# One two-layer mixer and expert kernel, its engines' work ordered by the list scheduler's timeline model instead of its coarse one

## The chip, the cores and the metric

The kernel runs on one core of a Trainium2 chip. The time is device microseconds of one execution; a smaller number is better. The core has a matmul engine (TensorE, in the rows PE, with PEld for its weight loads), VectorE (DVE), ScalarE (ACT), GpSimd (POOL) and SyncE (SP), which here only issues the DMA transfers. Each engine works through its own list of instructions in the order in which the built program holds them, and waits on semaphores where it needs another engine's result or a buffer.

## The reference

256 tokens `x` and 256 context tokens `ctx` of width 1024 run through two layers. Everything is float32.

```
for l in range(DEPTH):                      # 2 layers
    hl = _modulate(xl, norm1_g[l], shift, scale)     # the same for ctx
    pl = _split((hl @ w_in).astype(jnp.float32), IN_SIZES)
    a_l, a_c = _deltanet_branch(...)        # A: 4 heads, chunks of 64, triangular solve, scan both ways
    b_l, b_c = _gla_branch(...)             # B: 4 heads, chunks of 16, decays, scan both ways
    d_l, d_c = _diff_branch(...)            # C: softmax attention, p[0] - lam * p[1]
    y = (ga * (ya @ w_o_a) + gb * (yb @ w_o_b) + gd * (yd @ w_o_c)) @ w_out
    xl = xl + mod * y
    # layer 0: swiglu(h, w1, w3, w2), width 2816
    # layer 1: 8 experts of width 2816, the best 2 of each token
return _rmsnorm(xl, final_g)
```

## The kernel before

Activations lie with the model's width on the partitions, 512 tokens (context and `x`) beside each other. Weights come from HBM in pieces of 0.5 to 1 MB (`load`, L241 to L249) and are split for float32 accuracy: ScalarE copies the high part (L267), VectorE subtracts it to get the low part (L268), and a product is three matmuls (`mm3`, L272 to L274): high by high, high by low, low by high. In the first layers the two parts live in a tile `whl`, of which there are six; in the expert stage they are called `whi`, `wlo` and `wp`.

The function `mixer` writes the branches in the order of a plan, one string for each layer, for instance for layer 0:

```
"sm ap su pr iv ga4 m4 za sc m16 dec qkB gb1 ha ma vB gla qC kC m4 gc1 vC hb dif mb hc mc"
```

Here `ap`, `pr`, `iv` and `sc` are branch A: projections, preparation (`E` at L618, `U` at L622), the inverse of the triangular 32x32 blocks, and the scan over chunks. `iv` holds a chain of 31 steps on VectorE alone:

```
for c in range(31):
    a, b = 31 - c, c + 1
    nc.vector.tensor_mul(tv, N[:, c + 1:, c:c + 1]..., Y[:, c:c + 1, :b]...)   # L653
    nc.vector.tensor_sub(Y[:, c + 1:, :b], Y[:, c + 1:, :b], tv)               # L655
```

`gla` is branch B: eight iterations (four chunks of 128 tokens, two directions). Each builds decay factors (`F` on TensorE at L947 and L948, exponentials `Fe` on ScalarE at L950, products `zq` at L973 and `Fe` at L976 on VectorE), small matmuls `la` (L985), masked copies `ATb` from PSUM on VectorE (L987), and the outputs `ob` (L996, L998). `dif` is branch C, 16 heads of attention in layer 0 (scores at L1052, maxima at L1053, exponentials at L1056). The letters `g`, `z`, `h`, `m` and `m4` stand for gates, output gates, the output norm of a branch, its merge, and units of the modulation vectors (L348, L366): work of large projections that the branches don't wait for. In the text it is called filler, and so are the projections of the next branch (`qkB`, `vB`, `qC`, `kC`, `vC`).

The program order is only a priority. [...] After the mixer follow the dense layer (`ffn`) or, in layer 1, the experts (`turn` L1349 to L1356): 8 experts of 11 steps, each of which fetches 3 MB, casts it in six pieces on ScalarE and VectorE, and multiplies.

## Time and profile before

| what | value |
|---|---|
| median of 3 runs | 2604.94 us (2601.87 to 2605.57) |
| the profiled execution | 2607.5 us, its span 2605.7 us |
| busy share of the span | PE 94%, DVE 66%, ACT 54%, POOL 3% |
| mean granted TensorE clock | 0.962 of full |

The page lists for each engine its busy time, a picture of the span in 40 slices, and the chain of work that ended last. [...] A filler group of 24 matmuls of 512 columns needs two pairs of casts; TensorE works through it in about 5.4 us (24 by 227 ns) while the casts go on for the next.

### The profile page before, as it was taken

What the parts mean: (1) busy time and instruction counts of PE and PEld (TensorE: products, weight loads), DVE (VectorE), ACT (ScalarE), POOL (GpSimd) and SP (SyncE); (2) the same over time, 40 slices, a digit from 0 to 9 for tenths busy, and PEclk for the clock granted to TensorE, in tenths of its full rate; (3) what the DMA queues carried; (4) which work ended last, traced back from release to release, by engine and by line L of the source; (5) the groups of instructions that cost most, each with busy time, mean ns of one, the idle gap of its engine ahead of it and who ended that gap; (6) DMA issues with size and microseconds to landing.
All of it is one profiled execution on the core that took longest, in us unless ns stands there. A gap on an engine that the chain in (4) does not pass through costs nothing.

```text
span 2605.7 us, 35872 instructions
## 1 busy us (share of the span) xinstructions
PE 2455.8 (94%) x13712; PEld 1979.8 (76%) x13712; DVE 1718.3 (66%) x3130; ACT 1417.3 (54%) x2352; POOL 87.6 (3%) x216
## 2 busy tenths in 40 slices
PE   5998999999998999998979999998999999999997
PEld 3786777677677788886859878787878888878876
DVE  4675446655644533335686475767988888988987
ACT  3764343225553432334845432666878777777775
POOL 0000001110010000000000010010000000000000
PEclk8998999989999999998978999998999999999998
DMA  6323632022132223222273130246979899999994
GB/s 248 110 93 149 246 132 71 17 106 81 49 128 83 81 77 121 96 74 89 97 271 115 46 141 33 89 169 261 386 270 365 332 350 351 346 347 353 342 366 181
DMA packets 72707, 473.13 MB, mean 182 GB/s; under 512 B 8208, under 2 KB 10384, under 8 KB 19664
## 3 DMA queue, kind: packets, MB, share of 16 engines
q1 hardware_dynamic: 68208, 464.73, 48.1%
q10 hardware_dynamic: 4320, 6.03, 0.6%
q8 instruction: 110, 1.80, 0.3%
q14 instruction: 69, 0.57, 0.1%
HBM read 463.65 MB, written 7.08 MB: 181 GB/s over the span
## 4 chain that ended last, share of the span: by engine, by line
PE 85%; DVE 8%; ACT 4%; issue 2%; DMA 1%; SPq 0%; POOL 0%; ACTq 0%; DVEq 0%; POOLq 0%
PE pm L273 19%; PE pm L272 19%; PE pm L274 19%; PE y L274 3%; PE y L273 3%; PE y L272 3%; PE la L985 2%; PE pm L348 2%; PE pq L1052 1%; DVE ATb L987 1%; PE pm L844 1%; PE ob L996 1%; PE tp L1352 1%; DMA raw<-in_wmod_dram 1%; DVE zq L973 1%
## 5 line engine op out<-in xcount | busy, mean ns | idle before, releaser
L268 DVE TENSOR_TENSOR whl<-raw,whl 128x512 fp32r<-128x512 f32 (+2 forms) x490 | 331.2, 682 | 341.0 <-ACT whl L267 338.0
L272 PE MATMUL pm<-hh,whl 128*128 128x512 f32 (+2 forms) x1264 | 477.7, 380 | 13.0 <-ACT whl L267 6.6
L274 PE MATMUL pm<-hh,whl 128*128 128x512 f32 (+2 forms) x1264 | 467.7, 371 | 12.3 <-DVE whl L268 12.3
L267 ACT CAST whl<-raw 128x512 fp32r<-128x512 f32 (+2 forms) x490 | 289.8, 600 | 339.9 <-PE pm L274 268.7
L273 PE MATMUL pm<-hl,whl 128*128 128x512 f32 (+2 forms) x1264 | 470.9, 373 | 0.0
L268 DVE TENSOR_TENSOR wp<-rawc,wp 128x1024 fp32r<-128x1024 f32 x261 | 313.6, 1222 | 36.7 <-ACT wp L267 30.6
L272 PEld LDWEIGHTS pm<-hh,whl 128*128 128x128 f32 (+1 forms) x1264 | 244.8, 194 | 60.6 <-ACT whl L267 8.6
L274 PEld LDWEIGHTS pm<-hh,whl 128*128 128x128 f32 (+1 forms) x1264 | 243.5, 193 | 54.8 <-DVE whl L268 14.3
L267 ACT CAST wp<-rawc 128x1024 fp32r<-128x1024 f32 x261 | 268.1, 1051 | 21.1 <-PE y L274 11.5
L273 PEld LDWEIGHTS pm<-hl,whl 128*128 128x128 f32 (+1 forms) x1264 | 244.7, 194 | 42.6 <-issue 6.3
L268 DVE TENSOR_TENSOR wlo<-raw,whi 128x1024 fp32r<-128x1024 f32 x176 | 210.0, 1222 | 34.1 <-ACT whi L267 31.6
L273 PE MATMUL pm<-wlo,hg 128*128 128x512 f32 x530 | 211.8, 400 | 1.6 <-DVE wlo L268 1.4
L272 PE MATMUL pm<-whi,hg 128*128 128x512 f32 x530 | 211.2, 398 | 0.0
L274 PE MATMUL pm<-whi,hg 128*128 128x512 f32 x530 | 207.7, 392 | 0.0
L267 ACT CAST whi<-raw 128x1024 fp32r<-128x1024 f32 x176 | 179.0, 1052 | 13.2 <-PE pm L273 11.9
L273 PE MATMUL y<-wp,mt 128*128 128x512 f32 x348 | 135.4, 389 | 0.0
L274 PE MATMUL y<-wp,mt 128*128 128x512 f32 x348 | 135.3, 389 | 0.0
L273 PEld LDWEIGHTS pm<-wlo,hg 128*128 128x128 f32 x530 | 99.7, 188 | 34.6 <-DVE wlo L268 15.8
L272 PE MATMUL y<-wp,mt 128*128 128x512 f32 x348 | 120.1, 389 | 0.2 <-ACT mt L1354 0.2
L272 PEld LDWEIGHTS pm<-whi,hg 128*128 128x128 f32 x530 | 99.7, 188 | 20.9 <-ACT hg L1328 0.2
L274 PEld LDWEIGHTS pm<-whi,hg 128*128 128x128 f32 x530 | 99.7, 188 | 20.2
L268 DVE TENSOR_TENSOR wlo<-rawc,whi 128x1024 fp32r<-128x1024 f32 x91 | 110.9, 1219 | 1.9 <-ACT whi L267 1.3
(394 smaller groups left out, 4542.8 us busy)
## 6 DMA issues: line engine op xcount, KB each, us to landing
rawc<-in_m_dram SPq DMA_DIRECT2D x176, 1024.0 KB, 6.0
raw<-in_m_dram SPq DMA_DIRECT2D x88, 1024.0 KB, 7.4
raw<-in_win_dram SPq DMA_DIRECT2D x64, 1024.0 KB, 4.9
raw<-in_wmod_dram SPq DMA_DIRECT2D x40, 1024.0 KB, 5.0
raw<-in_f_dram SPq DMA_DIRECT2D x22, 1024.0 KB, 4.8
raw<-in_wo_dram SPq DMA_DIRECT2D x24, 512.0 KB, 3.7
raw<-in_f_dram SPq DMA_DIRECT2D x16, 704.0 KB, 4.0
rawc<-in_wmod_dram SPq DMA_DIRECT2D x8, 1024.0 KB, 16.9
```

Source lines behind the costliest of these rows:

```text
L267: self.nc.scalar.copy(hi, src)
L268: self.nc.vector.tensor_sub(lo, src, hi.bitcast(F32))
L272: mm(p, wh, ah, start=first, stop=False)
L273: mm(p, wh, al, start=False, stop=False)
L274: mm(p, wl, ah, start=False, stop=last)
L348: nc.tensor.matmul(p[j:j + 32, :256], self.cs[:, k, o:o + 32], w[:, k], start=i == 0 and k < 4, stop=i == n - 1 and k >= 4)
L844: nc.tensor.matmul(ps[:, :n], self.ones, sq[:, :n], start=True, stop=True)
L973: nc.vector.tensor_mul(FQ[hp][r, x, a].rearrange("p (n s) -> p n s", s=LEVELS[li]), side(Fj[:, x]), side(q[hp]))
L985: mm(p[:, x % 2, hp], FK[hp][:, x], FQ[hp][:, x], start=True, stop=True)
L987: nc.vector.copy_predicated(AT.rearrange("p h a (n t s) -> p (h a) n t s", t=2, s=s)[:, :, :, 1 - d], mk[:, None].to_broadcast([128, 4, 64 ...
L996: mm(o[:, hp], vB[:, tt, h * 128:(h + 1) * 128], AT[:, hp, a], start=True, stop=first)
L1052: mm(p[:, :nk], q[ms, h, cs], k[ms, h, :nk], start=True, stop=True)
```

## The change

One argument of the scheduler's context is set. The list scheduler then orders all engines' work with its timeline model (a time for every instruction, engine by engine) in place of its coarse one. The program handed to it, its priorities, buffers and instructions are the same; TensorE, VectorE, ScalarE and GpSimd have the same instructions before and after, in another order, and only the waits between engines are placed anew.

```
@@ -1565,7 +1565,7 @@
     out = nc.dram_tensor("out_0_dram", (128, 8, 256), F32, kind="ExternalOutput").ap()
-    with tile.TileContext(nc) as tc:
+    with tile.TileContext(nc, schedule_with_timeline_sim=True) as tc:
         program(tc, args, out)
```

Three places of the new order follow. The first is VectorE in `iv` of layer 0, the chain of L653 and L655. Before, its last steps and what stands behind it:

```order
L653 TENSOR_TENSOR fs<-W_1173 128x60
L655 TENSOR_TENSOR W_1173<-W_1173,fs 128x2x30
L653 TENSOR_TENSOR fs<-W_1173 128x31
L268 TENSOR_TENSOR whl<-raw,whl 128x512
L655 TENSOR_TENSOR W_1173<-W_1173,fs 128x31
L268 TENSOR_TENSOR whl<-raw,whl 128x512 x2
L658 COPY_PREDICATED W_1172<-mk,W_1173 128x1024
```

With the change the middle of the same chain reads so:

```order
L655 TENSOR_TENSOR W_1173<-W_1173,fs 128x22x10
L268 TENSOR_TENSOR whl<-raw,whl 128x512
L653 TENSOR_TENSOR fs<-W_1173 128x231
L268 TENSOR_TENSOR whl<-raw,whl 128x512 x2
L655 TENSOR_TENSOR W_1173<-W_1173,fs 128x21x11
L268 TENSOR_TENSOR whl<-raw,whl 128x512
L653 TENSOR_TENSOR fs<-W_1173 128x240
```

Before, one filler cast stands inside the 31 steps, just ahead of the last; with the change eight stand inside them, and three results of the gate `zs` (L807) too.

The second place is VectorE in an iteration of `gla` in layer 0, the seventh of eight. Before:

```order
L268 TENSOR_TENSOR whl<-raw,whl 128x512
L987 COPY_PREDICATED ATb<-mk,la 128x4x64
L268 TENSOR_TENSOR whl<-raw,whl 128x512
L973 TENSOR_TENSOR zq<-Fe,qkB 64x64 x7
L976 TENSOR_TENSOR Fe<-Fe,qkB 128x384
L973 TENSOR_TENSOR zq<-Fe,qkB 64x64 x5
L268 TENSOR_TENSOR whl<-raw,whl 128x512
L976 TENSOR_TENSOR Fe<-Fe,qkB 128x384
```

With the change:

```order
L973 TENSOR_TENSOR zq<-Fe,qkB 64x64 x6
L987 COPY_PREDICATED ATb<-mk,la 128x4x64
L976 TENSOR_TENSOR Fe<-Fe,qkB 128x384
L973 TENSOR_TENSOR zq<-Fe,qkB 64x64 x6
L976 TENSOR_TENSOR Fe<-Fe,qkB 128x384
L987 COPY_PREDICATED ATb<-mk,la 128x8x32
L987 COPY_PREDICATED ATb<-mk,la 128x16x16
```

The casts are gone from the last four iterations: the filler they belong to has been placed in the first four, and none is left. TensorE's list says the same: at the outputs of the fourth iteration it has 46 us more filler behind it than before (matmuls counted in both lists, at the start-to-start times of the trace, 227 ns for 512 columns and 120 ns for 256), and then no group until `gla` has ended.

The third place is ScalarE in the experts, one step of the sixth. `mt` (L1354) and `ms` (L1344) are the activations of the step, `whi` and `wp` weight casts. Before:

```order
L1354 CAST mt<-tp 128x256
L267 CAST wp<-rawc 128x1024 x2
L1344 ACTIVATE ms<-pm 128x256
L267 CAST wp<-rawc 128x1024
L267 CAST whi<-rawc 128x1024
L1328 CAST hg<-pm 128x512 x2
L267 CAST whi<-raw 128x1024 x2
```

With the change:

```order
L1354 CAST mt<-tp 128x256
L267 CAST whi<-raw 128x1024 x2
L1344 ACTIVATE ms<-pm 128x256
L1328 CAST hg<-pm 128x512 x2
L267 CAST wp<-rawc 128x1024 x3
L267 CAST whi<-rawc 128x1024
```

The pair of casts from `raw` moves from the end of the step to its start.

## Rows read from the trace of the kernel before

**Rows 1.** The page: busy time by engine, the chain that ended last.

```profile
PE 2455.8 (94%) x13712; PEld 1979.8 (76%) x13712; DVE 1718.3 (66%) x3130; ACT 1417.3 (54%) x2352; POOL 87.6 (3%) x216
...
PE 85%; DVE 8%; ACT 4%; issue 2%; DMA 1%; SPq 0%; POOL 0%; ACTq 0%; DVEq 0%; POOLq 0%
```

**Rows 2.** Windows of the span, from:to, length, busy by engine, PEclk, DMA share, GB/s.

```profile
150.00:200.00 50.00, 46.26 (x282) 37.19 (x281) 44.39 (x117) 27.12 (x42) 0.00 (x0) 0.99 0.33 114
200.00:250.00 50.00, 40.74 (x585) 32.90 (x582) 30.76 (x61) 27.55 (x44) 1.81 (x1) 0.84 0.29 108
...
900.00:1000.00 100.00, 100.00 (x443) 82.81 (x442) 36.74 (x61) 30.55 (x55) 0.00 (x0) 1.00 0.24 83
...
1350.00:1400.00 50.00, 38.04 (x635) 31.87 (x628) 38.96 (x82) 27.37 (x49) 1.81 (x1) 0.69 0.55 201
...
2400.00:2500.00 100.00, 99.33 (x456) 80.28 (x455) 90.60 (x102) 73.97 (x94) 0.00 (x0) 1.00 0.94 353
```

**Rows 3.** Timeline around the end of the inverse, layer 0 (start, us, what).

```profile
206.58 0.69 DVE L268 TENSOR_TENSOR whl<-raw,whl 128x512 fp32r<-128x512 f32 x1
...
207.32 0.80 PE L274 MATMUL pm<-hh,whl 128*128 128x512 f32 x1 [3.50 <-DVE whl L268]
```

**Rows 4.** Timeline of TensorE in the inverse of layer 1.

```profile
1367.80 0.58 PE L274 MATMUL pm<-hh,whl 128*128 128x256 f32 x1 [3.95 <-DVE whl L268]
```

**Rows 5.** Windows of `gla`, layer 0: four iterations, then single ones.

```profile
345.00:488.50 143.50, 133.69 (x722) 104.76 (x722) 85.78 (x251) 51.46 (x110) 13.41 (x58) 0.96 0.25 85
488.50:508.90 20.40, 19.42 (x104) 14.27 (x104) 15.47 (x56) 4.58 (x12) 3.68 (x15) 1.00 0.00 0
508.90:530.90 22.00, 19.51 (x141) 13.20 (x140) 13.49 (x50) 4.77 (x12) 3.02 (x14) 1.00 0.26 99
530.90:564.50 33.60, 32.55 (x147) 24.71 (x148) 19.16 (x62) 12.90 (x25) 3.42 (x15) 0.80 0.36 132
564.50:582.40 17.90, 16.59 (x117) 14.85 (x117) 11.57 (x44) 3.61 (x8) 2.31 (x10) 1.00 0.04 16
```

**Rows 6.** Groups of VectorE instructions, 345 to 584 us (busy, mean ns).

```profile
L973 DVE TENSOR_TENSOR zq<-Fe,qkB 64x64 f32<-64x64 f32 x224 | 40.8, 217 | 6.9 <-ACT Fe L950 2.6 <-PE tp L956 1.7 <-PE la L985 1.4
L987 DVE COPY_PREDICATED ATb<-mk,la 128x256 f32<-128x256 uint8 x56 | 29.1, 519 | 15.8 <-PE la L985 15.4
L268 DVE TENSOR_TENSOR whl<-raw,whl 128x512 fp32r<-128x512 f32 x40 | 27.1, 689 | 24.8 <-ACT whl L267 24.3
L976 DVE TENSOR_TENSOR Fe<-Fe,qkB 128x384 f32<-128x384 f32 (+1 forms) x48 | 22.2, 463 | 0.8
```

**Rows 7.** Chain of work at the end of the iteration 508.9 to 530.9.

```profile
525.59 0.47 DVE Fe L976
526.05 0.27 DVE zq L973 x2
...
527.58 0.47 PE la L985 x2
...
528.07 0.44 DVE ATb L987
...
530.07 0.73 DVE ATb L987
```

**Rows 8.** Groups of instructions in `dif`, layer 0, 600 to 725 us.

```profile
L1053 DVE TENSOR_REDUCE r<-pq 128x1 f32<-128x256 f32 (+1 forms) x32 | 17.2, 554 | 17.9 <-PE pq L1052 17.9
L1062 DVE SCALAR_TENSOR_TENSOR e<-e,r 128x256 f32<-128x256 f32 (+1 forms) x16 | 9.9, 616 | 0.4
...
L1056 ACT ACTIVATE e<-pq,r 128x256 f32<-128x256 f32 (+1 forms) x32 | 18.4, 579 | 17.1 <-DVE r L1054 17.1
```

**Rows 9.** Expert steps: the transposes L1352 of two stretches, first and last start.

```profile
L1352 PE MATMUL tp<-cstt,ms x19: 270/271/272, 1849.8 to 1925.6; 128*128 128x128 f32 x19
...
L1352 PE MATMUL tp<-cstt,ms x18: 270/271/272, 2512.9 to 2582.2; 128*128 128x128 f32 x18
```

**Rows 10.** Waits in the experts, 1850 to 2590 us (us, times, longest).

```profile
ACT ms L1344 <- PE pm L274: 76.9, 66, 2.4
...
PEld pm L273 <- DVE wlo L268: 15.8, 41, 0.9
```

**Rows 11.** VectorE's largest group in the experts (busy, mean ns).

```profile
L268 DVE TENSOR_TENSOR wp<-rawc,wp 128x1024 fp32r<-128x1024 f32 x244 | 292.9, 1222 | 31.5 <-ACT wp L267 26.4
```

More of the change, by code (lines that the diff above doesn't have):

```diff
@@ L1567 @@
     out = nc.dram_tensor("out_0_dram", (128, 8, 256), F32, kind="ExternalOutput").ap()
-    with tile.TileContext(nc) as tc:
+    with tile.TileContext(nc, schedule_with_timeline_sim=True) as tc:
         program(tc, args, out)
```

## The prediction

> **What bounds the kernel now.** I read the page first. TensorE is busy for 2455.8 of 2605.7 us and holds 85% of the chain that ended last, VectorE 8%, ScalarE 4% [rows 1]. An order can't take matmuls away, so all that it can win is the 150 us in which TensorE is idle, and what the lower clock costs. Next I read the windows, which say where these lie. The dense layer has no gap at all (100.00 of 100, clock 1.00), and the experts have next to none (99.33 of 100) [rows 2]. The losses sit in the mixers: around the inverse of branch A (40.74 of 50 us at clock 0.84 in layer 0, 38.04 at 0.69 in layer 1) [rows 2] and in `gla` [rows 5], where long chains on VectorE leave TensorE only filler. So the question is where the new order puts the filler, and I compared, at each milestone on TensorE, the filler that stands ahead of it in the two lists.
>
> **The inverse, layer 0.** Before, TensorE waits 3.50 us for a cast that VectorE does only at the end of its 31-step chain [rows 3], and then works on at the lower clock. With the change eight casts stand inside the chain, so this wait should go. The price: the chain becomes longer by 8 casts of 0.69 us [rows 6], and by three gates of about the same, some 7.5 us, and the join and the scan behind it come later by as much. Moreover TensorE's list has 12 to 19 us more filler ahead of the preparation, so that the chain also starts later. That is no loss by itself, since the filler has to be done at some time; but it is then missing behind the chain, in the first half of the scan. The window of the inverse loses 50 - 40.74 = 9.3 us of idle time and up to 0.16 x 50 = 8 us by the clock [rows 2], so at best 8 to 10 us come back of these 17; at worst the scan gets the same gaps (10 us more). I take **+2** (-8 to +10), nearer to the balance, since the gaps are moved rather than filled. In layer 1 the same wait (3.95 us) stands in the same place [rows 4], and the same move is made, with less filler left for the scan: **0** (-10 to +8).
>
> [...]
>
> **`gla`, layer 0.** This is the largest term. Eight iterations take 345 to 582 us. Before, each has 4 to 11 us of filler between its own steps, and some 15 us are left behind them. With the change the first four have all of it (46 us more than before, counted in the two lists), the last four have none. The last four took 20.4 + 22.0 + 33.6 + 17.9 = 93.9 us [rows 5]. What would they take bare? VectorE's own work is, for one iteration, 28 `zq` of 0.217, 7 `ATb` of 0.519 and 6 `Fe` of 0.463 us, 6.1 + 3.6 + 2.8 = 12.5 us [rows 6], and 1 us of small pieces, so 13.5; four are 54 us, the lower bound. The nearest measured iteration with little filler is the one of 508.9 to 530.9: about 4 us of filler and 22.0 us [rows 5]; the chain at its end goes from VectorE to TensorE and back, neither of them full [rows 7]. Four such are 88 us, the upper bound. The last iteration took 17.9 us with 8 us of filler, with TensorE busy for 16.59 of them [rows 5]; bare it can't be slower than that unless the clock falls, which makes 72. I take 76, a little above, because TensorE's own share (16.59 - 8 = 9 us of an iteration) leaves it idle for half of the time, and the clock fell right after the gaps of the iteration at 508.9: 0.80 in the next [rows 5].
>
> Against that stand the 46 us of filler and 4 us of modulation units that the last four no longer hold or that no longer follow them, and the stalls which the first four lose: 143.5 - 133.69 = 9.8 us idle and 0.04 x 143.5 = 5.7 us of clock [rows 5], of which I count 8. The old stretch with its filler behind it is 93.9 + 15 = 109 us, of which 50 move forward; so the bare four replace 59 us, and the term is 76 - 59 - 8 = **+9** (54 gives -13, 88 gives +21).
>
> [...]
>
> **`dif`, layer 0.** The filler there is also pulled forward, by up to 28 us: the last 7 of the 16 heads have no cast between them. A head needs on VectorE 2 x 0.554 + 0.616 + some 1.0 for its small pieces, 2.7 us, on ScalarE 2 x 0.579 and copies, 2.1 us [rows 8], and on TensorE about 3.4 us (its matmuls in the list at the trace's durations). TensorE would stay the bound of a bare head, if the heads overlap; the 17.9 us that `L1053` waits for scores and the 17.1 that the exponentials wait for maxima [rows 8] say that they overlap only in part. Seven heads at 0 to 1.2 us of gap: **+4** (0 to +8). For `gla` and `dif` in layer 1 the shift is smaller (only the last iteration of `gla` is bare): **+1** (-5 to +7).
>
> **The dense layer** keeps TensorE's order, row for row: 0. The first 60 us change a little, with loads in the same order: 0 (2 to either side).
>
> **The experts.** In the first experts a step takes (1925.6 - 1849.8) / 9 = 8.42 us, in the last one (2582.2 - 2512.9 - 0.3) / 8 = 8.63 [rows 9]. TensorE works all the time in the former; the latter carry a wait of `wlo`, 41 times and 15.8 us in all [rows 10], while VectorE is busy for 90.60 of 100 us [rows 2] with casts of 1222 ns [rows 11]. With the change the casts from `raw` come directly behind `mt`. Counted over the stage in the two lists, between the matmul that frees a cast's buffer and the one that first reads the new cast stand 6 to 7 us of matmuls in the median, where 4.1 to 4.5 stood. So most of the wait should go: 41 waits at 8.63 - 8.42 = 0.21 us of step each make 8.6. The new order is less regular, and `ms` on ScalarE, which already waits 76.9 us for its matmuls [rows 10], now has other casts queued behind it, which can cost a new wait. I take **-8** (-12 to +6).
>
> **The sum.** +2 + 0 + 9 + 4 + 1 - 8 = +8 us on the profiled 2607.5, 2615.5. The median of the runs shown is 2.6 us below that execution, so I forecast 2613.
>
> **The rivals.** *The bare tails run at VectorE's bound, and the covered chains pay* (the other side). The place is the last four iterations of `gla`: if the decay products, which don't depend on the scan's state, are ordered ahead well enough to keep VectorE full, they take 54 to 56 us instead of 76; the sum becomes 8 - 21 = -13 and the time 2592. It decides from about 67 us for the four downwards, where the sum is -1. For it: VectorE's order in these iterations has the `zq` of two groups in one run (x12). Against it: the 15.8 us in which `ATb` waits for `la` [rows 6]. *The bare tails lose the clock*: the four take 88 us (+21), `dif` +8, one inverse +6, experts -6: 2605 + 30 = 2635. For it: 0.80 and 0.69 after such gaps [rows 5, 2]; against it: the iteration at 508.9, which had the gaps, still ran at 1.00 itself [rows 5]. *No measurable change*: the gains of the experts and of the inverse equal the tails, or the chip's queues even it out, 2600 to 2610. For it: the dense layer and the experts, two fifths of the span, run at TensorE's own pace in either order.
>
> **How the numbers follow.** I give the forecast's case 0.36, the fast tails 0.28, the slow clock 0.19 and no change 0.17. About 0.2% (5 us) is what a measurement of this kernel can tell from no change. Of the forecast's case, whose own range is 2603 to 2625, about four fifths are slower by more than that and the rest is no change; so slower is 0.29 + 0.19 = 0.48, no change 0.07 + 0.12 = 0.19, faster 0.28 and 0.05 of the last case that falls below, 0.33. The range takes in most of both outer cases: 2584 to 2638.
>
> **What would show it.** Right: the wait of 3.5 us in the inverse is gone; the last four iterations of `gla` have no `whl` cast and TensorE busy for about half; `dif` ends with seven bare heads; the expert steps are 8.42 us to the end. Wrong: if the four bare iterations take under 65 us, or if the filler put ahead leaves new gaps in the scan or at the ends of branches, which I priced at little, or if the new order of the experts brings waits in place of the old ones; a step at 8.8 us there would alone cost 15 us.

## The result: 4.6% slower, and the profile after

With the change the kernel takes 2723.46 us (median of four runs, 2719.97 to 2730.92) against 2604.07 us (2601.87 to 2605.57): the ratio is 1.0463, 95% interval 1.044 to 1.0486. The profiled execution took 2719.97 us, its span is 2717.7 us, 112.0 more than before. The page of the profile after, its rows of busy time:

```profile
PE 2470.8 (91%) x13712; PEld 2020.1 (74%) x13712; DVE 1708.9 (63%) x3130; ACT 1420.4 (52%) x2352; POOL 88.5 (3%) x216
```

The work is the same as in [rows 1]; the mean granted clock fell from 0.962 to 0.932. To see where the time went, I cut both traces at the same milestones and took from each stretch the time that its matmuls need at their usual pace (for each shape the lower quartile of the distance from one start to the next, over both traces). What is left is time lost by TensorE, by waiting and by the clock. The sums differ by 111.4 us, so nothing is missing:

| stretch | lost before, us | lost after, us | more | predicted |
|---|---|---|---|---|
| start to the first output of `gla`, layer 0 | 110.6 | 117.2 | +6.6 | +2 |
| `gla`, iterations 1 to 4 | 19.4 | 16.0 | -3.4 | -8 |
| `gla`, iterations 5 to 8 | 28.6 | 74.6 | +46.0 | +17 |
| `dif` | 30.4 | 55.5 | +25.1 | +4 |
| output, norms, dense layer | 29.0 | 33.7 | +4.7 | 0 |
| layer 1, to the end of branch A | 71.2 | 81.7 | +10.5 | 0 |
| layer 1, `gla`, `dif`, output | 67.0 | 89.0 | +22.0 | +1 |
| experts | 55.7 | 55.6 | -0.1 | -8 |

The windows of the last four iterations of `gla` after, one row each (they answer to the last four of [rows 5]):

```profile
538.00:565.00 27.00, 18.40 (x77) 14.35 (x78) 14.44 (x52) 3.78 (x9) 3.55 (x15) 0.61 0.05 17
565.00:594.00 29.00, 19.31 (x67) 14.56 (x68) 12.42 (x47) 4.11 (x10) 3.02 (x14) 0.56 0.00 1
594.00:621.00 27.00, 19.28 (x72) 15.06 (x72) 12.94 (x48) 3.20 (x7) 3.41 (x15) 0.56 0.00 0
621.00:647.00 26.00, 16.60 (x59) 13.24 (x59) 11.97 (x46) 3.33 (x7) 2.31 (x10) 0.63 0.00 1
```

They are bare, as the order said: VectorE is busy for 12 to 14 us of each. But they take 26 to 29 us, 109 in all, where the forecast had 76, and TensorE is granted 0.56 to 0.63 of its clock. In windows of 1 us, 85 of these 109 read 0.50 and 16 read 1.00, so most of each iteration runs at 0.50 of its clock, which is meant by the lower clock here. Only 59 to 77 matmuls, small ones, keep it busy for 17 to 19 us. The chain of waits in one such iteration shows why there is no slack for a lower clock to hide in:

```profile
576.60 0.57 DVE Fe L976
577.17 0.14 issue
577.30 1.19 PE la L985 x4
...
584.49 0.57 DVE Fe L976
585.06 0.14 issue
585.20 1.63 PE la L985 x6
586.83 0.02 issue
586.85 0.43 DVE ATb L987
587.29 0.04 issue
587.33 1.24 PE la L985 x4
...
590.98 0.72 PE ob L998 x2
```

VectorE and TensorE take turns, one waiting while the other works, as at the end of an iteration in the kernel before [rows 7], but here through its middle too, and TensorE's turns are longer. In the kernel before, pieces of the same kind read so in the chain of waits of the iteration at clock 1.00 (508.9 to 530.9):

```profile
508.92 0.41 PE ob L998 x2
...
528.55 0.73 PE la L985 x4
```

Of the chain through all four bare iterations (538.9 to 647.8 us) TensorE holds some 67 us, VectorE 32. The bare heads of `dif` are a chain of the same kind (the chain of waits again):

```profile
779.77 0.68 DVE r L1053
780.47 0.16 DVE r L1054
780.66 0.78 ACT e L1056 x2
...
782.68 0.41 DVE e L1061
783.11 0.76 DVE e L1062
...
784.01 1.09 PE tp L1065 x4
785.10 2.06 PE pq L1052 x4
787.15 0.68 DVE r L1053
...
791.97 1.11 PE pq L1052 x4
793.08 0.67 DVE r L1053
```

From one `L1053` to the next pass 7.4 us: maxima, two exponentials, two scalings, transposes, and only then the next head's scores, since TensorE's list has them behind the transposes. All engines that I had added up side by side stand in one line here. The next head takes 5.9 us: its transposes and the scores behind them ran at a granted clock of 0.94 (791.3 to 793.1 us), those of the first at 0.50 (784.0 to 787.1 us).

### The profile page after: what moved, and what is told of

Read it like the earlier page. It is cut to its first block, busy times and chain, and to the rows that moved or that the text cites. A ratio compares the mean times of both kernels' runs of the same rounds, so it can differ in the third digit from the quotient of the medians.

```text
span 2717.7 us, 36061 instructions
## 1 busy us (share of the span) xinstructions
PE 2470.8 (91%) x13712; PEld 2020.1 (74%) x13712; DVE 1708.9 (63%) x3130; ACT 1420.4 (52%) x2352; POOL 88.5 (3%) x216
## 4 chain that ended last, share of the span: by engine, by line
PE 71%; DVE 6%; ACT 4%; issue 2%; DMA 1%; POOL 0%; ACTq 0%; DVEq 0%; POOLq 0%
PE pm L273 17%; PE pm L272 17%; PE pm L274 17%; PE y L274 3%; PE y L272 3%; PE y L273 3%; PE la L985 2%; PE ob L996 1%; PE pq L1052 1%; PE ob L998 1%; DVE zq L973 1%; PE pm L844 1%; DVE ATb L987 1%; PE tp L1352 1%; DMA raw<-in_wmod_dram 1%
## 5 line engine op out<-in xcount | busy, mean ns | idle before, releaser
L273 PE MATMUL pm<-hl,whl 128*128 128x512 f32 (+2 forms) x1264 | 464.8, 368 | 4.2 <-DVE hl L461 4.2
L268 DVE TENSOR_TENSOR wlo<-raw,whi 128x1024 fp32r<-128x1024 f32 x176 | 212.9, 1220 | 10.1 <-ACT whi L267 7.3
```

The lines of the kernel that those rows point to most:

```text
L268: self.nc.vector.tensor_sub(lo, src, hi.bitcast(F32))
L273: mm(p, wh, al, start=False, stop=False)
```

## Experiments

Nine of the ten kernels hold an engine's list to an order that is written into the kernel, by dependencies between neighbours of a list that bring no wait. All but the last of the ten were run once, and runs of one kernel differ here by up to 11 us (2719.97 to 2730.92 for the change). The edit is the same for all of them, with other lists, and stands ahead of the dense layer or of the experts:

```
+def _pin(tc, nc):
...
+            if last is not None:
+                tc.add_manual_dep(have[name], last, why, reason="pin")
+            last = name
...
+                _pin(self.tc, self.nc)
                 self.ffn(x, H)
```

Theory A says that the place of the filler in TensorE's list costs the time; theory B says that the order on VectorE and ScalarE inside the chains does, where casts and long runs of `zq` now stand.

**All lists of layer 0 as before** (lists of all five engines up to the dense layer).

> Timeline model, but every engine's list for layer 0 up to the dense layer is held to the order of the kernel before. Both theories (filler placed too early; or worse order on VectorE and ScalarE inside the chains) expect the 77 to 80 us that the dense layer starts late to go: 2717 - 79 = 2638 us, within 8. If the loss came from somewhere else (other waits, other addresses of the buffers), it stays above 2690.

It took 2639.89 us (before, on the same chip, 2604.03): 84 us came back, 80 against the profiled execution of the change. The whole loss of layer 0 is in the order; no change of addresses or waits outside it is needed to explain it.

**Only TensorE's list as before.**

> Timeline model; in layer 0 up to the dense layer only TensorE's list is held to the order of before, VectorE and ScalarE are ordered by the timeline model around it. Theory A (the place of the filler on TensorE decides) expects 2638 to 2655 us. Theory B (the order on VectorE and ScalarE inside the chains decides) expects 2690 us or more.

2659.2 us. TensorE's order alone brings 64 of the 84 us; the other 20 come back only with the other engines' lists.

**The reverse: coarse model, TensorE's list of the change.**

> The reverse: the coarse model, but in layer 0 up to the dense layer TensorE's list is held to the order of the change. Theory A expects 2604 + 79 = 2683 us, within 12. Theory B expects at most 2625 us.

2699.65 us, 96 us slower than before: more than theory A expected, and 75 more than theory B allows. The output matmuls of `gla` in layer 0 (L996; durations, then first and last start) in the change:

```profile
L996 PE MATMUL ob<-ATb,vB x64: 270/377/580, 419.4 to 647.8; 128*128 128x128 f32 x64
```

The same in this reverse:

```profile
L996 PE MATMUL ob<-ATb,vB x64: 270/399/580, 435.7 to 663.6; 128*128 128x128 f32 x64
```

And with only TensorE as before:

```profile
L996 PE MATMUL ob<-ATb,vB x64: 274/276/582, 420.8 to 598.4; 128*128 128x128 f32 x64
```

From the first output to the last, TensorE's list of the change gives 228 us with either order on VectorE; its list of before gives 178 with the change's order around it, and 167 in the kernel before (416.7 to 583.4). Some 19 of the 61 us between 228 and 167 are work and no loss: matmuls that stood elsewhere before (the two `gla` stretches of the table, less what is lost in them, are 118 us before and 137 after). The four bare iterations of the reverse take 107.3 us at 0.56 to 0.63, as in the change (windows, the first and the last of the four):

```profile
555.60:582.70 27.10, 18.76 (x77) 14.43 (x77) 13.78 (x51) 3.79 (x9) 3.54 (x15) 0.61 0.04 16
...
637.50:662.90 25.40, 17.34 (x58) 13.52 (x57) 12.00 (x45) 3.49 (x7) 2.31 (x10) 0.57 0.00 1
```

So the price of a bare iteration doesn't come from VectorE's order. Theory B stands only for the smaller part. The parts don't add up, either: TensorE's new list costs 96 us alone and 80 with the change's other lists. The 16 us lie ahead of the first output of `gla` (435.7 here, 419.4 in the change). So the new order of VectorE and ScalarE costs some 20 us around the old list of TensorE and saves some 16 around the new one.

**Where in layer 0: from branch B's decays on, TensorE's list as before; branch A free.**

> Timeline model; of layer 0 only what is written from the decays of branch B on (gla, dif, merges and their filler) is held to the order of before on TensorE; branch A's preparation, inverse and scan with their filler are free. If the bare tails of gla and dif are the loss and branch A is near to neutral, as the prediction had it (+2), this takes what holding all of TensorE's list took: 2659 us, within 8. If the early filler around the inverse costs time of its own, it takes 2670 us or more.

2674.57 us: 15 more than with all of TensorE's list held. The first output of `gla` comes at 436.4 in place of 420.8, and from there `gla` takes as long, 178 us (L996 in this kernel):

```profile
L996 PE MATMUL ob<-ATb,vB x64: 275/275/377, 436.4 to 614.5; 128*128 128x128 f32 x64
```

The early filler around the inverse is not neutral: where the later order is the same, it costs 15 us. These 15 us can't be counted as part of the 84: in the change itself the first output comes at 419.4, and up to there only 6.6 us more are lost than before (the table).

**Is it the clock? Extra matmuls in `gla`, lists left free.**

```
+                            if l == 0 and g == 1 and x % 2 == 0:
+                                with self.tc.issue_after(la.ins):
+                                    warm = self.pm()
+                                    for _ in range(6):
+                                        mm(warm[:, :384], G[tt][:, 0, gs], w384, start=True, stop=True)
```

> The change, with 30 extra matmuls of 384 columns (results unused) in each of the last four iterations of gla in layer 0, six behind each group of la. If the lower clock is what makes these iterations 27 us long, the clock there rises to over 0.85 and the four take 80 to 92 us in place of 109: 2695 to 2705 us. If it is the chain between VectorE and TensorE whatever the clock, the extra matmuls (about 5 us in each iteration at the full clock) only add: 2725 to 2745 us.

2784.19 us. This tells nothing about the clock: with the extra matmuls the scheduler made another order of the whole layer (the second to fourth iteration take 23 to 29 us in it, 37 to 44 in the change). So I put extra matmuls into the change's own order, all lists of layer 0 held.

**128 extra matmuls in the gaps, order held.**

```
+                            for _ in range(10 if l == 0 and g == 1 and j and x == 0 else 0):
+                                mm(p[:, 0, 0], G[tt][:, 0, :128], self.wl[:, d, :128], start=True, stop=True)
...
+                            for _ in range(12 if l == 0 and g == 1 and a == 0 else 0):
+                                mm(o[:, 0], G[tt][:, 0, :128], self.wl[:, d, :128], start=True, stop=True)
```

> The change, with every engine's list in layer 0 held to the change's own order, and 10 to 12 extra matmuls of 128 columns (results overwritten) directly ahead of each of 12 matmuls that wait for VectorE in the last four iterations of gla: 128 in all, at 0.165 us each 21 us of work at the full clock. If the lower clock makes up most of what a bare iteration costs beyond VectorE's work, the clock there rises to over 0.85 and the four iterations take 82 to 95 us in place of 109: 2695 to 2706 us. If the chain between the engines costs as much at either clock, the extra work is added to it: 2725 to 2745 us.

2723.87 us: neither. The clock of the four iterations rose to no more than 0.57 to 0.73, so the question stayed open; the extra matmuls, some 23 us as they ran, cost nothing.

**288 extra matmuls** (24 at each place).

> As the pinned run with 128 extra matmuls, but 24 in place of 10 or 12 at each of the 12 places: 288, 48 us of work at the full clock, enough to fill each gap of 3.5 to 4.6 us. If the clock makes the bare iterations long, it now rises to 0.9 or more and the four iterations take 85 to 100 us in place of 107: 2700 to 2715 us. If it doesn't rise, the matmuls run at half rate, 7 us at each place, and the four iterations take 125 us or more: 2735 us or more.

2708.41 us, 15 us faster than the change (12 less than its fastest run) with some 37 us more for TensorE to do. At the full clock 24 extra matmuls take 2.7 us, 0.113 us each and not the 0.165 of the expectations. The four iterations take 94.6 us (543.8 to 638.4, from the last output matmul of the fourth to that of the eighth, `L996` before) and the clock is back:

```profile
538.00:564.00 26.00, 22.85 (x164) 20.32 (x163) 17.39 (x57) 6.49 (x14) 3.55 (x15) 0.93 0.07 22
564.00:590.00 26.00, 22.87 (x156) 19.68 (x156) 12.68 (x48) 4.11 (x10) 3.02 (x14) 0.93 0.00 1
590.00:615.00 25.00, 22.24 (x160) 18.90 (x160) 13.34 (x49) 3.82 (x9) 3.71 (x17) 1.00 0.00 1
615.00:640.00 25.00, 22.57 (x132) 20.40 (x131) 12.39 (x48) 3.22 (x7) 2.02 (x8) 0.80 0.00 1
```

So the lower clock makes at least 14 of the 109 us. The remaining 24 us for an iteration are near to the 22.0 of the iteration that I had taken as the upper bound [rows 5]. How much of these 24 is the extra work itself isn't separated here. At seven of the twelve places TensorE goes on from the last extra matmul without a gap, and the extra matmuls hold 22 us of the chain of waits of the four. Without them, at the clock of these windows, the four would take between 73 and 95 us, so the clock makes between 14 and 36 of the 109.

An estimate from the rows of the result falls between: a piece of `la` took 0.73 us at the full clock and 1.24 bare, one of `ob` 0.41 and 0.72. TensorE's 67 us of the bare chain would so become 39 at the full clock, and the 109 us 81.

In all four bare iterations the granted clock is 0.56 to 0.63, and with the waits filled it is 0.80 to 1.00.

**The same for `dif`** (20 more ahead of the transposes of each bare head).

```
+                for _ in range(20 if l == 0 and qt >= 2 and (qt > 2 or h) else 0):
+                    mm(tp[:, 0], self.ones, self.ones, start=True, stop=True)
```

> As the pinned run with 288 extra matmuls in gla, and 20 more of 128 columns (results overwritten) ahead of the transposes of each of the seven heads of dif that have no filler, 140 in all. A bare head is a chain of some 8.3 us, of which TensorE holds about 4.8 at the lower clock. If the clock is a part of its price, TensorE's share halves and the seven heads take 40 to 47 us in place of 58: 2692 to 2700 us, against 2708 without them. If not, 2708 to 2730 us.

2708.21 us: no difference in the time. The clock of the bare heads went from 0.64 (window of the run with 288, without extra matmuls in `dif`)

```profile
738.00:795.00 57.00, 33.97 (x110) 19.45 (x110) 20.14 (x55) 17.45 (x42) 0.00 (x0) 0.64 0.13 53
```

to 0.94 (the same window with them). TensorE is now busy for 51 of the 57 us, most of it with the extra matmuls.

```profile
738.00:795.00 57.00, 51.43 (x381) 42.11 (x379) 21.48 (x56) 19.87 (x46) 0.00 (x0) 0.94 0.13 52
```

The heads did become shorter. Their maxima (`L1053` before), in the run with 288 and then here:

```profile
L1057 DVE TENSOR_REDUCE r<-pq x14: 680/686/692, 736.6 to 783.4; 128x1 f32<-128x512 f32 x14
...
L1057 DVE TENSOR_REDUCE r<-pq x14: 679/686/692, 736.5 to 779.7; 128x1 f32<-128x512 f32 x14
```

That is 46.8 us and 43.2: most heads take 6.2 to 7.05 us in place of 7.3. The 3.6 us are lost again behind `dif`, within what runs differ by. And the extra work has itself become the limit (the chain of waits here; the 20 matmuls of a head stand as 40 in the trace):

```profile
772.86 4.47 PE tp L1069 x40
777.33 0.44 PE tp L1071 x4
777.77 1.06 PE pq L1056 x4
778.83 1.09 PE oc L1075 x8
```

These make 7.06 us, and TensorE doesn't wait between them. So the clock's share in the 25 us of `dif` is at least 3.6 us; how much more stays open. An estimate: in the chain of the change, transposes and scores of a head take 1.09 + 2.06 us at the lower clock, 0.44 + 1.06 here, so 1.65 us less for a head, some 10 to 12 of the 25. That a bare head has room for 20 extra matmuls at no cost is shown.

**The experts alone in the new order** (both mixers and the dense layer as before).

> Timeline model, with every engine's list held to the order of before in both mixers and the dense layer; only the experts and the end are in the timeline model's order. The prediction's own term for the experts (-8) expects 2596 us. The trace of the change (88 steps in 774.3 us against 774.2) expects no difference: 2604 us, within 4.

2608.05 us against 2603.48 on the same chip. The experts' steps span the same time in both (transposes L1352, first and last start, in this kernel):

```profile
L1352 PE MATMUL tp<-cstt,ms x176: 270/271/330, 1809.5 to 2582.6; 128*128 128x128 f32 x176
```

773.1 us, and 774.3 before (1807.9 to 2582.2): the new order gains 1 us there, not 8. The 4.6 us more of one run each are near to what two runs can differ by. Against the run with layer 0 alone held (2639.89) 32 us came back, so the loss of layer 1 (10.5 + 22.0 in the table) is in the order too.

**A version that might beat both: before, with extra matmuls around the inverse.** If gaps cost clock, filling them in the kernel before could pay: 132 matmuls at seven places, all lists up to the experts held to the order of before.

```
+    def warm(self, p):
+        self.warmed += 1
+        for _ in range(WARM.get(self.warmed, 0)):
+            self.nc.tensor.matmul(p[:, :128], self.ones, self.C("ident"), start=True, stop=True)
```

> The kernel before (coarse model, every list held to its own order up to the experts), with 132 extra matmuls of 128 columns (results unused) at seven places where TensorE waits around the inverse of branch A in both layers. If a lower clock behind such gaps costs time that the gaps themselves don't, this is faster: 2592 to 2600 us. If not, the same within 3 us of 2604, or slower where the extra matmuls delay a group: up to 2612 us.

2617.86 us against 2605.29, ratio 1.0051 (1.0033 to 1.0068): slower. The clock rose (two windows of the inverse in layer 1 below, 0.83 and 0.91, where 1350 to 1400 had 0.69 [rows 2]), and the first output of `gla` in layer 0 came 0.5 us earlier, but that of layer 1 came 7 us later. In layer 1 the 96 extra matmuls took 23 us as they ran, and TensorE's waits around them (1300 to 1460 us) fell only from 21 to 18 us: most of the extra work was added to the waits and did not fill them, and the higher clock gave back only a part of it. Filling that meets the waits themselves is not tested. So a higher clock alone was no gain here, and no experiment points to an order that beats the one before.

```profile
1350.00:1370.00 20.00, 15.22 (x159) 11.22 (x158) 11.07 (x31) 3.86 (x8) 0.00 (x0) 0.83 0.72 267
...
1390.00:1410.00 20.00, 17.16 (x504) 15.85 (x505) 14.39 (x28) 17.14 (x34) 1.80 (x1) 0.91 0.23 74
```

## Why the prediction was wrong, step by step

**The direction and the largest places were right, the prices were not.** The range ended at 2638; the time is 85 us above it.

**`gla`, layer 0: the step that failed first.** "The nearest measured iteration with little filler ... Four such are 88 us, the upper bound." That iteration ran at clock 1.00 with 4 us of filler, so it was no bound for one with none. Bare, the clock stays low through all four iterations, 0.56 to 0.63: 109 us where I took 76, and +42.6 for the term (+46.0 - 3.4) in place of +9. By the estimate above the four would take some 81 us at the full clock, inside my bounds of 54 to 88. So the term fell short mostly by the clock, and by how much is an estimate; shown are 14 us. My sentence that a bare last iteration "can't be slower than that unless the clock falls" held the answer; I then priced the case of the low clock with an iteration at the full one. The rival of the slow clock had the right mechanism, and its 2635 the same wrong price, 88.

**`dif`, layer 0.** "Seven heads at 0 to 1.2 us of gap" was worked out from each engine's sum, as if heads overlapped. They don't: from one of the seven bare heads to the next pass 7.3 to 7.4 us four times, once 9.4 and once 5.9, where TensorE has 2.6 us to do at the full clock (0.44 + 1.06 + 1.09 in the run above; my 3.4 was too much). +25.1 instead of +4. The waits of 17.9 and 17.1 us [rows 8] were the warning; with filler beside them they cost little (TensorE was busy for 119 of those 125 us), so they looked small.

**Layer 1.** "... the shift is smaller (only the last iteration of `gla` is bare)", +1. That iteration is bare indeed, 29 us at 0.52 (its window after), against 25 at 0.93 before; but a part of the +22.0 lies in the iterations ahead of it and at the start of the stage, and branch A cost 10.5 more, which I had put at 0.

```profile
1710.00:1739.00 29.00, 19.80 (x65) 15.55 (x65) 12.35 (x46) 3.36 (x7) 2.31 (x10) 0.52 0.00 1
```

In branch A the join waits 10.8 us for the last copy of the inverse, where no such wait stood before (the waits of TensorE, 1400 to 1555 us):

```profile
PE v L699 <- ACT W L677: 10.8, 1, 10.8
```

**The inverse, layer 0.** The step was right as far as it went: the wait of 3.50 us [rows 3] is gone, and the 31 steps take 30.0 us from the first `L655` to the last in place of 23.4, 6.6 more where I had 7.5. The casts and gates inside the chain brought few waits: of the eight casts one waited, for 0.37 us, and two of the three gates, 0.9 us together. But other waits come instead. TensorE now waits 10.1 us for modulation weights (the waits of TensorE, 185 to 300 us), 3.7 before, which I had not counted, and 7.1 us for a copy of the next branch (300 to 350 us).

```profile
PE pm L348 <- DMA raw<-in_wmod_dram: 10.1, 4, 4.3
...
PE pm L272 <- ACT qkB L875: 7.1, 1, 7.1
```

The gaps that I had given as the scan's worst case did come, TensorE being idle for 16.4 us there (windows, before and after):

```profile
300.00:350.00 50.00, 49.94 (x261) 37.86 (x260) 20.91 (x34) 23.41 (x43) 0.00 (x0) 0.93 0.46 159
...
300.00:350.00 50.00, 33.63 (x215) 27.83 (x214) 20.97 (x37) 16.95 (x31) 0.00 (x0) 0.90 0.06 18
```

The whole stretch lost 6.6 us more, inside the term's range.

**The experts.** The waits for `wlo` did go, as forecast: they no longer appear among the waits of TensorE or its weight loads, and the middle (median) step takes 8.43 us in place of 8.63. But TensorE's own waits rose from 4.2 to 12.4 us, most of it for `mt` at the outputs (waits, 1962 to 2700 us; the answer to [rows 10]):

```profile
ACT wp L267 <- PE y L274: 100.9, 99, 4.3
...
ACT ms L1344 <- PE pm L274: 9.6, 8, 3.4
...
PE y L272 <- ACT mt L1354: 5.6, 9, 1.5
```

Before, the outputs waited 0.2 us for `mt`. I had named a new wait behind `ms`, at +6 at most; it came behind `mt`, and with it the stage takes 774 us as before. What ScalarE itself waits says little: 76.9 us at `ms` became 9.6, and 8.7 at the casts for the output matmuls became 100.9, but all its waits together are 182 us before and 178 after. What holds up `mt` was not tested. The dense layer was as predicted, within 2 us of loss.

**What stays open.** Why the timeline model lays so much filler into the first four iterations of `gla` was not tried; nor how the prices of the bare iterations and of `dif`'s bare heads divide between the clock and the chain, beyond the bounds and estimates above.

## What to carry to other kernels

Here work that nobody waits for was worth more beside the last chain than beside the first (the first four iterations of `gla` lost 3.4 us less with more of it, the last four 46.0 more without): count, for each chain, the filler that is still left when it starts. Price an uncovered chain as a line of waits from engine to engine with TensorE at the clock that bare stretches show (0.56 to 0.63 here), not by the busiest engine's sum (13.5 us of VectorE for an iteration that took 26 to 29), and take no iteration that still has filler as a bound for one that has none (22.0 us with some 4 of it). An order that keeps TensorE busier now can be the slower one, here by 4.6%.

## What was not expected of the hardware

TensorE did some 37 us more work and the kernel became 15 us faster: 288 extra matmuls raised the granted clock of four iterations from between 0.56 and 0.63 to between 0.80 and 1.00. With 128 of them the clock stayed at 0.57 to 0.73 and the time didn't change.
